# Moving the tiles of a tuned encoder layer to multiples of 512 bytes in SBUF

## The chip, the core and the metric

The kernel runs on one core of a Trainium2 chip. The metric is device time in microseconds, from the first to the last instruction of one execution with what lies around it; runs of one kernel are summed up by their median. SBUF is the on-chip memory: 128 partitions, each a strip of bytes. A tile lies at the same byte in every partition, and "place" below means that byte. TensorE (PE) multiplies matrices and loads the stationary operand of the next matmul (PEld) beside the running one; VectorE (DVE), ScalarE (ACT) and GpSimd (POOL) work on tiles; SyncE (SP) issues most DMAs.

## The reference

One encoder layer on 256 rows of width 2048, all in float32:

```
x <- LN1(alpha*x + 0.5*SwiGLU_1(x))      2048 -> 2 x 5632 -> 2048
x <- LN2(alpha*x + W_out [Hyena(x) ; DiffAttn(x)])
x <- LN3(alpha*x + 0.5*SwiGLU_2(x))
```

SwiGLU is `(silu(x Wg) * (x Wu)) Wd`. The mixer in the middle projects x by one matrix of 6144 columns: 3072 for Hyena (a short convolution, then two long convolutions whose filters come from a small sine network), 3072 for differential attention with 8 heads; both halves go through one output matrix. LN is a layer norm with gain and bias.

## The kernel before, in words

Every large product is made in float32r from operands that are split in two: a high part (a cast on ACT) and a low part (the rest, subtracted on DVE). Three products hi·hi, hi·lo and lo·hi stand for one float32 product.

All weights stream through SBUF in units of 512 KB, 128 x 1024 floats. `fetch` (L155) sends a unit into one of 4 buffers `raw`; `prepare` casts it into one of 4 buffers `whi` (names `hi...`, L171) and subtracts into one of 4 buffers `wlo` (names `lo...`, L172). The list `units` fixes their order, five units are fetched and two are prepared ahead of use. There are three kinds of stage:

- The gate stages (L368, L369) and the Hyena projection hold the activations `xx` (16 blocks of 2 x 256, high and low side by side) as the moving operand; a weight part is the stationary one. For each 128 columns of weights the high part meets all 512 columns of a block of `xx`, the low part the first 256.
- The down stages, the attention projection and the output projection (`mm3`, L90 to L92) hold a weight part as the moving operand, 512 columns, and `hh`/`hl` (or `xx`, `yhh`, `yah`) as the stationary one. In the last down stage four of the last eight units are prepared into `xx` itself, which is free by then, instead of `whi` and `wlo`.
- Beside these, generators that `tick` advances do the small work: the filter network (`filter_net`, L475 to L502) and the filters' spectra in the first FFN, the Hyena chains and the heads in the mixer. They take scratch tiles of 2 KB from a ring of eight, `t512`.

The order of instructions on each engine is the scheduler's: an instruction whose inputs are there early may be put far ahead of its place in the source. Tiles come from pools that lie one after the other in SBUF: `const`, `wp` (the units), `sm` (scratch), then the pools of a stage (`hh` and `hl`; `ssq`, `yah` and the rest of the mixer). A pool is filled in the order in which its tiles are first made, so every tile's size moves all that comes after it.

| tiles | place before | past a multiple of 512 | place now | past a multiple of 512 |
|---|---|---|---|---|
| `res` | 16512 | 128 | 18944 | 0 |
| `xx` | 32896 | 128 | 35328 | 0 |
| `ident`, `ones` | 65664, 66176 | 128 | 16896, 17408 | 0 |
| `pvt0`, `pvt1` | 66720, 67232 | 160 | 17920, 18432 | 0 |
| `raw` (4 of 4096) | from 67936 | 352 | from 68096 | 0 |
| `whi`, `wlo` (8 of 4096) | from 84320 | 352 | from 84480 | 0 |
| `t512` (8 of 2048) | from 117088 | 352 | from 117248 | 0 |
| `hf`, `sg` (4 of 1024) | from 133472 | 352 | from 134016 | 384 |
| `hh` | 139168 | 416 | 138752 | 0 |
| `hl` | 184224 | 416 | 183808 | 0 |
| mixer: `ssq`, `yah`, `yal`, `rope` | from 139168 | 416 | from 138752 | 0 |
| mixer: the rest (`qk`, `fw_hi`, `iv`, `yhh`, ...) | from 159712 | 480 | from 159232 | 0 |

Of the kernel before, what the change touches and what calls it, by code (L numbers as in the profile page):

```python
# [11 lines left out]
F32 = mybir.dt.float32  # L12
# [5 lines left out]
P = 128  # L18
# [9 lines left out]
EMB = 33  # L28
HID = 64
# [45 lines left out]
def kernel(ctx: ExitStack, tc: tile.TileContext, a: dict, out: bass.AP):  # L75
    nc = tc.nc

    const = ctx.enter_context(tc.tile_pool(name="const", bufs=1))
    wp = ctx.enter_context(tc.tile_pool(name="wp", bufs=4))
    sm = ctx.enter_context(tc.tile_pool(name="sm", bufs=2))  # L80
# [2 lines left out]

    def bank(name):
        return psp.tile([P, 512], F32, tag="ps", name=name)

    mm = nc.tensor.matmul

# [16 lines left out]
    def t512(name, shape=(2, CH)):  # L105
        return sm.tile([P, *shape], F32, tag="t512", name=name, bufs=T512)
# [105 lines left out]
            tick()  # L212


    res = const.tile([P, 2, D], F32, name="res")
    xx = const.tile([P, KD, 2, L], F32R, name="xx")
    xv = a["x"][0].rearrange("(p j) d -> p j d", j=2)
# [4 lines left out]
        if kp % 2 == 0:  # L222
            fetch(kp // 2 + 1)

    ident = const.tile([P, P], F32, name="ident")
    make_identity(nc, ident)
    ones = const.tile([P, P], F32, name="ones")
    nc.gpsimd.memset(ones, 1.0)
    mhalf = const.tile([P, 2], F32, name="mhalf")
    nc.gpsimd.memset(mhalf, -0.5)  # L230


    NCONV = 24
    NV = 4 * KD
    pvt = [const.tile([P, P], F32, name="pvt0"), const.tile([P, P], F32, name="pvt1")]

    def load_vectors():
        pv = [sm.tile([P, P], F32, tag="hf", name=f"pv{i}") for i in range(2)]
        for w in range(3):
            nc.gpsimd.dma_start(out=pv[0][w * NCONV:(w + 1) * NCONV, :], in_=a["hyena_conv_w"][0, w].rearrange("(t p) -> t p", p=P))  # L240
        nc.gpsimd.dma_start(out=pv[0][3 * NCONV:4 * NCONV, :], in_=a["hyena_conv_b"][0].rearrange("(t p) -> t p", p=P))
        r = 0
        for nme in ("ln1_g", "ln1_b", "ln2_g", "ln2_b"):
            nc.gpsimd.dma_start(out=pv[1][r:r + KD, :], in_=a[nme][0].rearrange("(t p) -> t p", p=P))
            r += KD
        nc.gpsimd.dma_start(out=pv[1][r:r + 8, :], in_=a["hyena_norm_g"][0].rearrange("(t p) -> t p", p=P))
        nc.gpsimd.dma_start(out=pv[1][r + 8:r + 9, :], in_=a["subln_g"])
        yield 4
        for i, n in ((0, 4 * NCONV), (1, NV + 9)):
            ps = bank(f"ps_pv{i}")  # L250
            nc.tensor.transpose(out=ps[:, :n], in_=pv[i][:n, :], identity=ident[:n, :n])
            nc.vector.tensor_copy(out=pvt[i][:, :n], in_=ps[:, :n])
# [11 lines left out]
    def xt_chunk(tag, c, g, b):  # L264
        for kp in (2 * c, 2 * c + 1):
            hs = xx[:, 2 * kp:2 * kp + 2, 0, :]
            ls = xx[:, 2 * kp:2 * kp + 2, 1, :]
            if g is None:
                i1 = nc.scalar.copy(out=hs, in_=xt0[kp])
                i2 = sub(nc.vector, ls, xt0[kp], hs)  # L270
                if c == 0:
                    hold["act"], hold["dve"] = i1, i2
                continue
            ps = bank(f"ps_xt{tag}_{kp}")
            for i in range(2):
                k = 2 * kp + i
                for j in range(2):
                    nc.tensor.transpose(out=ps[:, i * L + j * P:i * L + (j + 1) * P], in_=res[:, j, k * P:(k + 1) * P], identity=ident)  # L278
            t = t512(f"xt{tag}_{kp}")
            for i in range(2):  # L280
                k = 2 * kp + i
                i1 = nc.scalar.activation(out=t[:, i, :], in_=ps[:, i * L:(i + 1) * L], func=AF.Identity, bias=ln_col(b, k), scale=ln_col(g, k))  # L282
                if kp == 0:
                    nc.vector.tensor_copy(out=hs[:, i, :], in_=t[:, i, :])
                    i2 = sub(nc.vector, ls[:, i, :], t[:, i, :], hs[:, i, :])
            if kp > 0:
                nc.vector.tensor_copy(out=hs, in_=t)
                i2 = sub(nc.gpsimd if kp in (3, 5, 7) else nc.vector, ls, t, hs)
            if kp == 1:
                hold["act"], hold["dve"] = i1, i2  # L290

    def warm(n):

        ps = bank("ps_warm")
        for _ in range(n):
            mm(out=ps[:, :P], lhsT=ones, rhs=ones, start=True, stop=True)

    def scale_residual(tag, g, b):

        for c in range(4):  # L300
# [11 lines left out]
            for j in range(2):  # L312
# [2 lines left out]
                yield 1  # L315
                nc.vector.scalar_tensor_tensor(out=r, in0=bt, scalar=ALPHA, in1=r, op0=ALU.mult, op1=ALU.add)
                yield 1

    stats = const.tile([P, 2, 4, 6], F32, name="stats")

    def add_rows(ps, j, c, scale):
        cs = slice(c * 512, (c + 1) * 512)
# [150 lines left out]
    def filter_net():  # L473
        zt = t512("zt", (512,))[:EMB, :L]
        nc.sync.dma_start(out=zt, in_=a["c_zt"])  # L475
        w1 = sm.tile([EMB, HID], F32, name="w1", tag="w1", bufs=1)
        nc.sync.dma_start(out=w1, in_=a["filt_w1"][0])
        w2 = sm.tile([HID, HID], F32, name="w2", tag="w2", bufs=1)
        nc.sync.dma_start(out=w2, in_=a["filt_w2"][0])
        w3 = sm.tile([HID, 2, HID], F32, name="w3", tag="w3", bufs=1)  # L480
        fb = sm.tile([P, 4], F32, name="fb", tag="fb", bufs=1)
        for h in range(2):
            nc.sync.dma_start(out=w3[:, h, :], in_=a["filt_w3"][0])
            for i, nme in enumerate(("filt_b1", "filt_b2", "filt_b3", "filt_freq")):
                nc.gpsimd.dma_start(out=fb[h * HID:(h + 1) * HID, i:i + 1], in_=a[nme][0].rearrange("(h o) -> h o", o=1))
        yield 6

        def sine(o, ps, i, n, tag):
            ar = sm.tile([P, L], F32, tag="sg", name=f"ar{tag}")[:n]
            nc.vector.tensor_scalar(out=ar, in0=ps, scalar1=fb[:n, i:i + 1], scalar2=fb[:n, 3:4], op0=ALU.add, op1=ALU.mult)  # L490
            kn = sm.tile([P, L], F32, tag="hf", name=f"kn{tag}")[:n]
            nc.vector.tensor_scalar(out=kn, in0=ar, scalar1=1.0 / (2.0 * math.pi), scalar2=MAGIC, op0=ALU.mult, op1=ALU.add)
            nc.vector.tensor_scalar(out=kn, in0=kn, scalar1=-MAGIC, scalar2=None, op0=ALU.add)
            for c in (C1, C2, C3):
                nc.vector.scalar_tensor_tensor(out=ar, in0=kn, scalar=-c, in1=ar, op0=ALU.mult, op1=ALU.add)
            nc.vector.tensor_scalar(out=ar, in0=ar, scalar1=PI_LO, scalar2=-PI_LO, op0=ALU.min, op1=ALU.max)
            nc.scalar.activation(out=o, in_=ar, func=AF.Sin)

        h = zt
        for i, (w, n) in enumerate(((w1, HID), (w2, HID), (w3.rearrange("a b c -> a (b c)"), P))):  # L500
            ps = bank(f"ps_f{i}")
            mm(out=ps[:n, :L], lhsT=w, rhs=h, start=True, stop=True)  # L502
            h = t512(f"fh{i}", (512,))[:n, :L]
            yield 1
            sine(h, ps[:n, :L], i, n, f"f{i}")
            yield 3
        flt["h"] = h
# [97 lines left out]
    def rows_of_x():  # L605
# [4 lines left out]
        yield from scale_residual("0", None, None)  # L610

    ln = ffn("1", first0, filter_gen(), filter_net(), fill)
    xn1 = dr.tile([P, 2, D], F32, name="xn1")

# [13 lines left out]
    mixp = mix.enter_context(tc.tile_pool(name="mix", bufs=1, reuse_waits="tile"))  # L628
# [202 lines left out]
    yah = mixp.tile([P, 8, L], F32R, name="yah")  # L831
    yal = mixp.tile([P, 8, L], F32R, name="yal")
    rope = mixp.tile([P, 2, 2, 8, ROT], F32, name="rope")
    nlam = mixp.tile([P, 1], F32, name="nlam")
    g08 = mixp.tile([P, 1], F32, name="g08")

    def lambdas():
        nc.sync.dma_start(out=rope.rearrange("p a j g r -> p (a j g r)"), in_=a["c_rope"])
# [221 lines left out]
```

## Time and profile before

| | before |
|---|---|
| median of 3 runs | 1960.94 us (1959.08 to 1961.29) |
| the profiled execution | 1963.29 us, of it 1961.2 us span |
| granted TensorE clock, mean | 0.995 |
| PE busy | 1932.8 us, 99% of the span, 10260 matmuls |
| DVE, ACT, POOL busy | 62%, 47%, 16% |
| DMA moved | 376.43 MB, mean 192 GB/s |

A group's row of the profile reads: line, engine, operation, output<-inputs by the program's names, partitions x elements, count | busy us in all, mean ns of one | idle us just before and what ended it. Ends of matmuls are modelled, so their pace is better read from the starts in a timeline. In the table of waits a row says who waited for whom, us in all, how often, and the longest.

### The profile page before, as it was taken

What the parts mean: (1) busy time and instruction counts of PE and PEld (TensorE: products, weight loads), DVE (VectorE), ACT (ScalarE), POOL (GpSimd) and SP (SyncE); (2) the same over time, 40 slices, a digit from 0 to 9 for tenths busy, and PEclk for the clock granted to TensorE, in tenths of its full rate; (3) what the DMA queues carried; (4) which work ended last, traced back from release to release, by engine and by line L of the source; (5) the groups of instructions that cost most, each with busy time, mean ns of one, the idle gap of its engine ahead of it and who ended that gap; (6) DMA issues with size and microseconds to landing.
All of it is one profiled execution on the core that took longest, in us unless ns stands there. A gap on an engine that the chain in (4) does not pass through costs nothing. (4 is left out here: it accounts for less than half of the span.)

```text
span 1961.2 us, 27062 instructions
## 1 busy us (share of the span) xinstructions
PE 1932.8 (99%) x10260; PEld 1656.4 (84%) x10260; DVE 1215.4 (62%) x1538; ACT 926.1 (47%) x1334; POOL 305.3 (16%) x330
## 2 busy tenths in 40 slices
PE   9999999999999999999999999999999999999997
PEld 8888888888888887888887878888888888888885
DVE  5555556555566656899978666755555555544445
ACT  5554444544444435545555534545444544433332
POOL 4221111121100002012222011312111121100001
PEclk9999999999999999999999999999999999999999
DMA  8656656656666656655575444865656556555553
GB/s 288 204 187 192 190 189 198 192 185 193 203 208 214 204 191 207 220 181 153 172 226 161 158 154 157 274 191 187 192 191 193 187 189 194 187 189 187 189 186 115
DMA packets 294698, 376.43 MB, mean 192 GB/s; under 512 B 13263, under 2 KB 222312, under 8 KB 294568
## 3 DMA queue, kind: packets, MB, share of 16 engines
q1 hardware_dynamic: 289832, 361.90, 57.6%
q0 software_dynamic: 4736, 12.82, 2.2%
q8 instruction: 80, 1.31, 0.3%
q14 instruction: 50, 0.41, 0.1%
HBM read 366.27 MB, written 8.39 MB: 191 GB/s over the span
## 5 line engine op out<-in xcount | busy, mean ns | idle before, releaser
L368 PE MATMUL ps<-xx,hi1g 128*128 128x512 f32 x1408 | 490.2, 391 | 1.5 <-ACT hi1g L171 1.5
L368 PE MATMUL ps<-xx,hi2g 128*128 128x512 f32 x1408 | 488.6, 390 | 1.1 <-DVE xx L95 1.1
L369 PE MATMUL ps<-xx,lo1g 128*128 128x256 f32 x1408 | 397.4, 283 | 0.1
L369 PE MATMUL ps<-xx,lo2g 128*128 128x256 f32 x1408 | 397.0, 282 | 0.0
L172 DVE TENSOR_TENSOR lo2g<-raw2g,hi2g 128x1024 fp32r<-128x1024 f32 x176 | 234.8, 1335 | 179.6 <-ACT hi2g L171 179.6
L172 DVE TENSOR_TENSOR lo1g<-raw1g,hi1g 128x1024 fp32r<-128x1024 f32 (+1 forms) x178 | 232.5, 1308 | 177.6 <-ACT hi1g L171 177.6
L368 PEld LDWEIGHTS ps<-xx,hi1g 128*128 128x128 f32 x1408 | 264.8, 188 | 58.2 <-ACT hi1g L171 1.7
L368 PEld LDWEIGHTS ps<-xx,hi2g 128*128 128x128 f32 x1408 | 264.3, 188 | 56.4 <-ACT xt L282 1.3
L171 ACT CAST hi2g<-raw2g 128x1024 fp32r<-128x1024 f32 x176 | 185.0, 1052 | 187.3 <-PE ps L368 174.9
L171 ACT CAST hi1g<-raw1g 128x1024 fp32r<-128x1024 f32 (+1 forms) x178 | 185.2, 1042 | 179.7 <-PE ps L368 170.7
L369 PEld LDWEIGHTS ps<-xx,lo1g 128*128 128x128 f32 x1408 | 266.7, 190 | 0.7 <-DVE lo1g L172 0.5
L369 PEld LDWEIGHTS ps<-xx,lo2g 128*128 128x128 f32 x1408 | 266.1, 189 | 0.1
L404 POOL TENSOR_TENSOR hf<-hf,sg 128x256 f32<-128x256 f32 x88 | 64.7, 755 | 741.8 <-DVE hf L373 741.7
L172 DVE TENSOR_TENSOR lo2d<-raw2d,hi2d 128x1024 fp32r<-128x1024 f32 x84 | 103.6, 1233 | 118.7 <-ACT hi2d L171 118.7
L171 ACT CAST hi1d<-raw1d 128x1024 fp32r<-128x1024 f32 x88 | 92.4, 1050 | 132.0 <-PE pd L92 119.7
L171 ACT CAST hi2d<-raw2d 128x1024 fp32r<-128x1024 f32 x84 | 88.4, 1052 | 138.7 <-PE pd L92 131.0
L172 DVE TENSOR_TENSOR lo1d<-raw1d,hi1d 128x1024 fp32r<-128x1024 f32 x88 | 107.2, 1221 | 72.7 <-ACT hi1d L171 72.7
L90 PE MATMUL pd<-hi1d,hh 128*128 128x512 f32 x352 | 139.3, 396 | 0.0
L368 PE MATMUL ph<-xx,hihy 128*128 128x512 f32 x384 | 137.0, 397 | 2.2 <-DVE xx L95 1.1
L92 PE MATMUL pd<-hi1d,hl 128*128 128x512 f32 x352 | 139.1, 395 | 0.0
L91 PE MATMUL pd<-lo1d,hh 128*128 128x512 f32 x352 | 139.1, 395 | 0.0
L90 PE MATMUL pd<-hi2d,hh 128*128 128x512 f32 x336 | 132.9, 395 | 0.0
(380 smaller groups left out, 3078.8 us busy)
## 6 DMA issues: line engine op xcount, KB each, us to landing
raw1d<-in_ffn_w_down_dram SPq DMA_DIRECT2D x88, 512.0 KB, 4.3
raw2g<-in_ffn_w_gate_dram SPq DMA_DIRECT2D x88, 512.0 KB, 3.5
raw2g<-in_ffn_w_up_dram SPq DMA_DIRECT2D x88, 512.0 KB, 3.5
raw2d<-in_ffn_w_down_dram SPq DMA_DIRECT2D x88, 512.0 KB, 4.2
raw1g<-in_ffn_w_gate_dram SPq DMA_DIRECT2D x87, 512.0 KB, 3.5
raw1g<-in_ffn_w_up_dram SPq DMA_DIRECT2D x87, 512.0 KB, 3.9
rawhy<-in_w_in_dram SPq DMA_DIRECT2D x48, 512.0 KB, 4.5
rawat<-in_w_in_dram SPq DMA_DIRECT2D x48, 512.0 KB, 4.2
```

The lines of the kernel that those rows point to most:

```text
L90: mm(out=o, lhsT=lh, rhs=rh, start=start, stop=False)
L91: mm(out=o, lhsT=lh, rhs=rl, start=False, stop=False)
L92: mm(out=o, lhsT=ll, rhs=rh, start=False, stop=stop)
L171: i1 = nc.scalar.copy(out=hi[:, s_], in_=raw[:, s_])
L172: i2 = nc.vector.tensor_tensor(out=lo[:, s_], in0=raw[:, s_], in1=hi[:, s_].bitcast(F32), op=ALU.subtract)
L368: mm(out=ps[t], lhsT=h[:, k, ts_], rhs=xx[:, kk].rearrange("p a l -> p (a l)"), start=kk == 0, stop=False)
L369: mm(out=ps[t][:, :L], lhsT=lo[:, k, ts_], rhs=xx[:, kk, 0, :], start=False, stop=kk == KD - 1)
L404: nc.gpsimd.tensor_tensor(out=hf, in0=hf, in1=sg, op=ALU.mult)
```

## The change

No arithmetic is changed. The constants that are small (`mhalf`, `stats`) and those of 512 bytes (`ident`, `ones`, the two `pvt`) are made first, with a spacer behind the small ones; the spacers `space` are tiles that nothing reads or writes. `sm` gets a spacer of 384 bytes, which makes its length such that the next pool begins on a multiple of 512. Three tiles of the filter network (`w1`, `w2`, `w3`, 256, 256 and 512 bytes) become pieces of one scratch tile `fw` of the ring `t512`. `nlam` and `g08`, 4 bytes each, go from the mixer's pool to `sm`.

```diff
+    def line(pool, n):
+
+        pool.tile([P, n // 4], F32, name="space", tag="space", bufs=1)
...
+    mhalf = const.tile([P, 2], F32, name="mhalf")
+    stats = const.tile([P, 2, 4, 6], F32, name="stats")
+    line(const, 384 - 32 - 192)
+    ident = const.tile([P, P], F32, name="ident")
+    ones = const.tile([P, P], F32, name="ones")
+    pvt = [const.tile([P, P], F32, name="pvt0"), const.tile([P, P], F32, name="pvt1")]
...
     res = const.tile([P, 2, D], F32, name="res")
     xx = const.tile([P, KD, 2, L], F32R, name="xx")
...
-    ident = const.tile([P, P], F32, name="ident")
+    line(sm, 384)
     make_identity(nc, ident)
-    ones = const.tile([P, P], F32, name="ones")
     nc.gpsimd.memset(ones, 1.0)
-    mhalf = const.tile([P, 2], F32, name="mhalf")
     nc.gpsimd.memset(mhalf, -0.5)
...
-    pvt = [const.tile([P, P], F32, name="pvt0"), const.tile([P, P], F32, name="pvt1")]
...
-    stats = const.tile([P, 2, 4, 6], F32, name="stats")
...
-        w1 = sm.tile([EMB, HID], F32, name="w1", tag="w1", bufs=1)
+        ws = t512("fw", (512,))
+        w1, w2 = ws[:EMB, :HID], ws[:HID, HID:2 * HID]
+        w3 = ws[:HID, 2 * HID:4 * HID].rearrange("p (a b) -> p a b", a=2)
         nc.sync.dma_start(out=w1, in_=a["filt_w1"][0])
-        w2 = sm.tile([HID, HID], F32, name="w2", tag="w2", bufs=1)
         nc.sync.dma_start(out=w2, in_=a["filt_w2"][0])
-        w3 = sm.tile([HID, 2, HID], F32, name="w3", tag="w3", bufs=1)
...
-    nlam = mixp.tile([P, 1], F32, name="nlam")
-    g08 = mixp.tile([P, 1], F32, name="g08")
+    nlam = sm.tile([P, 1], F32, name="nlam", tag="nlam", bufs=1)
+    g08 = sm.tile([P, 1], F32, name="g08", tag="g08", bufs=1)
```

On four engines the order of instructions stays as it was. On DVE one instruction moves: the product that makes `g08` (printed as `g`) from a column of `pvt`. Before, its tile shared bytes with the first FFN's `hh`, and it stood at the end of that FFN, between the sum of the last rows and their statistics:

```order
L323 SCALAR_TENSOR_TENSOR res<-pd_3_1_6239,res 128x512 [waits PE_49]
L851 TENSOR_SCALAR g_8514<-pvt_107 128x1 [waits Pool_49]
L324 BN_STATS stats<-res 128x6 [waits DVE_49]
L328 BN_AGGR mv_6678<-stats 128x2 [waits DVE_49]
L330 TENSOR_SCALAR rs_6680<-mv_6678 128x1 [waits DVE_49]
```

Now it stands near the start of the program, right behind the copy that fills `pvt`, in front of the low part of a unit:

```order
L261 COPY pvt_74<-ps_pv_404 128x96 [waits PE_49]
L261 COPY pvt_75<-ps_pv_407 128x73 [waits PE_49]
L858 TENSOR_SCALAR g_8514<-pvt_75 128x1 [waits DVE_49]
L176 TENSOR_TENSOR lo1g_2_0_429<-raw1g_2_0_330,hi1g_2_0_428 128x1024 [waits DMAHW6_49,Activation_49]
L380 TENSOR_TENSOR hf_0_366<-ps_0_1_0_136,hf_0_366 128x256 [waits DMASW2_49,DMASW1_49,DMASW3_49,DMASW0_49,Activation_49]
```

The rows at the end of the first FFN are otherwise as before.

## The prediction, made before the changed kernel was run

> **What bounds the kernel now.** I read the page's busy table and its groups first, then the table by stage, then the waits of PE, and last single stretches of the timeline. The profiled execution took 1963.29 us, 2.35 us over the median of the runs (1960.94); its span is 1961.2 us, and 2.1 us lie around it.
>
> ```profile
> PE 1932.8 (99%) x10260; PEld 1656.4 (84%) x10260; DVE 1215.4 (62%) x1538; ACT 926.1 (47%) x1334; POOL 305.3 (16%) x330
> ```
>
> The table by stage (us, then busy us of each engine with its count, granted clock, DMA share, GB/s) has PE without a gap in both FFNs:
>
> ```profile
> 0.00:60.00 60.00, 57.31 (x313) 50.73 (x314) 36.23 (x41) 34.22 (x49) 31.62 (x42) 0.97 0.87 278
> 60.00:630.00 570.00, 570.00 (x3141) 495.79 (x3140) 330.23 (x368) 272.06 (x390) 84.41 (x94) 1.00 0.61 195
> 630.00:760.00 130.00, 130.00 (x577) 105.61 (x576) 72.35 (x77) 52.34 (x55) 3.20 (x7) 1.00 0.61 197
> 760.00:960.00 200.00, 192.53 (x1126) 169.65 (x1125) 180.90 (x335) 109.54 (x176) 39.36 (x34) 0.98 0.59 187
> 960.00:1210.00 250.00, 245.97 (x1217) 201.27 (x1216) 181.38 (x306) 119.37 (x210) 41.20 (x41) 1.00 0.54 173
> 1210.00:1870.00 660.00, 660.00 (x3567) 571.68 (x3566) 365.73 (x365) 311.85 (x431) 97.19 (x107) 1.00 0.61 195
> 1870.00:1961.00 91.00, 76.95 (x330) 61.63 (x328) 48.57 (x51) 26.77 (x26) 8.28 (x6) 0.95 0.44 148
> ```
>
> So PE is idle for 28 us: 2.7 at the head, 11.5 in the mixer (7.5 + 4.0), 14 at the end. The rest, 1933 us, is the pace of the matmuls, and only that pace is large enough to be measured in this kernel: 0.2% of the time, which I take as the least that can be told from no change, is 3.9 us, or 0.38 ns on each of 10260 matmuls. The question is whether a place in SBUF changes that pace.
>
> **The change, part by part: the matmuls.** The kernel before already has operands at four different places: 128 bytes past a multiple of 512 (`xx`), 352 (the units), 416 (`hh`, `hl`) and 480 (most of the mixer). If place mattered, like operations should differ between them. The groups, kept apart by shape:
>
> ```profile
> L91 PE MATMUL pd<-lo2d,hh 128*128 128x512 f32 x336 | 132.9, 395 | 0.0
> L91 PE MATMUL pd<-xx,hh 128*128 128x512 f32 x16 | 6.3, 395 | 0.0
> L90 PEld LDWEIGHTS pd<-hi2d,hh 128*128 128x128 f32 x336 | 63.2, 188 | 15.3
> L90 PEld LDWEIGHTS pa0k<-hiat,xx 128*128 128x128 f32 x32 | 6.0, 188 | 1.4
> L91 PEld LDWEIGHTS pwo<-lowo,yhh 128*128 128x128 f32 x64 | 12.1, 189 | 2.6
> L368 PEld LDWEIGHTS ps<-xx,hi2g 128*128 128x128 f32 x1408 | 264.3, 188 | 56.4 <-ACT xt L282 1.3
> ```
>
> A stationary operand loads in 188 or 189 ns from 416, 128, 480 and 352 alike. For the moving operand the ends are modelled, so I take the starts. In the last down stage 24 matmuls read a unit that was prepared into `xx` (128), the next 24 one from the ordinary buffers (352), and then 24 from `xx` again:
>
> ```profile
> 1924.41 0.40 PE L90 MATMUL pd<-xx,hh 128*128 128x512 f32 x1
> 1930.00 0.40 PE L90 MATMUL pd<-hi2d,hh 128*128 128x512 f32 x1
> 1935.60 0.40 PE L90 MATMUL pd<-xx,hh 128*128 128x512 f32 x1
> 1941.20 0.39 PE L90 MATMUL pd<-hi2d,hh 128*128 128x512 f32 x1
> ```
>
> 5.59, 5.60 and 5.60 us for 24 each: 0.233 us for one, and a difference of at most 0.01 us in 24, 0.4 ns each. 128 is a multiple of 64 and 352 is not, so any rule with pieces of up to 32 bytes, or of 64, is seen to cost nothing. What no row shows is a start on a whole 512 (or 256): all four places cross one more such border than an aligned operand does. The cost of that crossing has to be bounded. From above in time: nothing lost. From below: at most what separates the slower matmuls from the faster ones, which I price as a rival. The nearest rows are the three stretches just shown, so I take 0, with 0.4 ns each way as the plain uncertainty: 3072 matmuls of 512 columns in the down, attention and output products (2112, 576 and 384 by the loops) by 0.4 ns are 1.2 us, and over all 10260 it would be 4.1 us.
>
> [...]
>
> **DVE, ACT and POOL.** Their operations move with their operands:
>
> ```profile
> L172 DVE TENSOR_TENSOR lo1d<-raw1d,hi1d 128x1024 fp32r<-128x1024 f32 x88 | 107.2, 1221 | 72.7 <-ACT hi1d L171 72.7
> L172 DVE TENSOR_TENSOR xx<-raw2d,xx 128x1024 fp32r<-128x1024 f32 x4 | 4.9, 1221 | 1.7 <-ACT xx L171 1.6
> L171 ACT CAST hi2d<-raw2d 128x1024 fp32r<-128x1024 f32 x84 | 88.4, 1052 | 138.7 <-PE pd L92 131.0 <-DMA raw2d<-in_ffn_w_down_dram 4.3 <-PE ps L368 3.5
> L171 ACT CAST xx<-raw2d 128x1024 fp32r<-128x1024 f32 x4 | 4.2, 1052 | 2.2 <-DMA raw2d<-in_ffn_w_down_dram 2.2
> ```
>
> Writing to 352 or to 128 takes the same 1221 and 1052 ns. Even a change here would lie beside PE: DVE idles for 42 to 45 of every 100 us in the FFNs, and ACT waits mostly for PE to free the weight buffers. In the mixer, where DVE is busy for 181 of 200 us, a change of 1% in its operations would move the 7.5 idle us of PE by up to 1.8 us; I take 0.
>
> **The transfers.** Rows of 1 to 2 KB now land at whole multiples of 512. If they came faster, it would show where PE waits for a unit or its input. These are the waits of PE, whole:
>
> ```profile
> PE py L90 <- ACT rha L98: 1.9, 1, 1.9
> PE pw L923 <- DVE e L919: 1.6, 1, 1.6
> PE py L91 <- DVE rla L95: 1.5, 1, 1.5
> PE ps L368 <- ACT hi1g L171: 1.5, 1, 1.5
> ...
> PE ph L369 <- DVE lohy L172: 0.5, 1, 0.5
> ```
>
> Only the 1.5 us at the head has a transfer behind it (the first unit). A tenth off the 3.5 us (its row is below) in which a gate unit lands is 0.35 us, so the gain is 0 to 0.4 us; I take 0.1. With the cover gone it would be one landing per unit, but the covers are five units of lead.
>
> ```profile
> raw2g<-in_ffn_w_gate_dram SPq DMA_DIRECT2D x88, 512.0 KB, 3.5
> ```
>
> **The moved instruction.** `g08` leaves the end of the first FFN, where PE goes idle for the statistics:
>
> ```profile
> 760.65 0.69 DVE L323 SCALAR_TENSOR_TENSOR res<-pd,res 128x512 f32<-128x512 f32 x1 [0.49 <-PE pd L92]
> 761.38 0.69 DVE L324 BATCH_NORM_STATS2 stats<-res 128x6 f32<-128x512 f32 x1
> 763.45 0.69 DVE L323 SCALAR_TENSOR_TENSOR res<-pd,res 128x512 f32<-128x512 f32 x1 [0.89 <-PE pd L92]
> 764.05 0.14 DVE L851 TENSOR_SCALAR g<-pvt 128x1 f32<-128x1 f32 x1
> 764.17 0.69 DVE L324 BATCH_NORM_STATS2 stats<-res 128x6 f32<-128x512 f32 x1
> ```
>
> From the sum to the statistics it is 0.73 us for the other half of the rows, without `g08`, and 0.72 with it: it sat in the wait of the statistics for the sum, so its removal gives 0, at most 0.14. Where it goes now, DVE has 0.18 us of waiting for ACT, and what is queued behind it is the low part of a unit that PE uses two units later:
>
> ```profile
> 35.71 0.39 DVE L252 COPY pvt<-ps_pv 128x96 f32<-128x96 f32 x2
> 36.28 1.23 DVE L172 TENSOR_TENSOR lo1g<-raw1g,hi1g 128x1024 fp32r<-128x1024 f32 x1 [0.18 <-ACT hi1g L171]
> ```
>
> Cost there: 0 to 0.14 us on DVE, 0 on PE.
>
> **The filter's weights in the ring.** `fw` is one more tile in a ring of eight, so the scratch tiles of the filters' side work change places and a few of their waits. It is side work of the first FFN, whose stages have PE busy in 570 of 570 and 130 of 130 us. I take 0, with 0.5 us each way for its three small matmuls, which stand in PE's own row. The spacers cost nothing: no instruction touches them.
>
> **The sum**: matmuls 0 (up to 1.2 us each way, 4.1 at the very most), transfers −0.1 (−0.4 to 0), side work 0 (0.5 each way), the mixer 0 (1.8 each way), `g08` 0 (−0.14 to 0). From 1963.29 the profiled execution would go to 1963.2, and the median from 1960.9 to 1960.8; no change beyond what can be told. The runs before span 2.2 us by themselves.
>
> **The rivals.** A, faster: crossings cost something and go. Starts give a price. Gate pairs (512 and 256 columns), and matmuls of 256 columns alone:
>
> ```profile
> 299.87 0.39 PE L368 MATMUL ps<-xx,hi1g 128*128 128x512 f32 x1
> 301.95 0.39 PE L368 MATMUL ps<-xx,hi1g 128*128 128x512 f32 x1
> 763.24 0.28 PE L90 MATMUL prk<-xx 128*128 128x256 f32 x1
> 765.40 0.28 PE L90 MATMUL pik<-xx 128*128 128x256 f32 x1
> ```
>
> Six pairs in 2.08 us are 0.347 each; 18 matmuls of 256 columns in 2.16 are 0.120 each; so 512 columns take 0.227 in a gate, where the moving tile lies at 128, and 0.233 in a down stage, where it lies at 352. If that 6 ns were the place, 3072 by 6 ns, 18 us, would go: 1942. Against it stand the 24 with a moving operand at 128 that run at 0.233 too. For it: nothing but that 512 itself is untried. Chance 0.09, somewhat smaller gains included. [...]
>
> B, slower: operands that began at different places within 512 bytes now begin at the same one, and the load of the stationary operand meets the reading of the moving one in the same part of the memory. The place is the gate stage (`xx` at 128 against units at 352 before, both at 0 now). The price is the slower pace that the kernel knows, 0.233 for 0.227: 3200 pairs of the gates and of Hyena's projection (2816 and 384) by 6 ns, 19 us, 1980; it decides from 1.2 ns a pair. Against it: `prk<-xx` above has both operands in `xx`, at equal places already, and its 256 columns take 0.120 us, only 3 ns over half of the 0.233 that 512 take with operands at 416 and 352. Chance 0.07.
>
> C, the transfers or the mixer's chains change by more than I give them: 1 to 3 us either way, 1958 to 1964, still no change. Chance 0.10.
>
> D, the places do not become what the change says: `hf` and `sg` in fact stay 384 past a multiple of 512. They only feed DVE, ACT and POOL, so the time is the same; it is part of the forecast.
>
> **How the numbers follow.** Forecast 0.69 (with D), C 0.10, A 0.09, B 0.07, and 0.05 for effects of unknown sign. Same: the forecast and nearly all of C, 0.77; faster: A and half of the unknown, 0.13; slower 0.10. The likeliest case alone lies in 1958 to 1964. The range is 1954 to 1966: it takes in C and the smaller effects on either side, and leaves out A and B at full size, under 2 in 10.
>
> **What would show it.** Right: the groups L368 to L369 and L90 to L92 at 390, 283 and 395 ns as before, starts 0.347 and 0.233 apart, LDWEIGHTS at 188, PE busy near 1933. A shows as a down pace below 0.233, B as a gate pair above 0.347. Transfers show in the median landing of `raw2g` against 3.5 us, with PE's waits unchanged. I am wrong if the pace of the matmuls moves by more than 0.4 ns each.

## The result, and the profile after

The changed kernel takes 1947.22 us (median of 4 runs, 1945.09 to 1950.04) where the kernel before took 1961.12 beside it (4 runs, 1959.08 to 1962.32): a ratio of 0.9931, with an interval of 0.9914 to 0.9948. It is faster by 13.9 us, where no change was forecast, and lies outside the range of 1954 to 1966. The profiled execution, from which all that follows is read, took 1945.09 us against 1963.29: 18.2 us less, with a span of 1943.3 us against 1961.2 and the same mean clock of 0.996 and 0.995.

The busy table and two rows of the table by stage, same windows and columns as before:

```profile
PE 1914.9 (99%) x10260; PEld 1644.5 (85%) x10260; DVE 1215.8 (63%) x1538; ACT 927.2 (48%) x1334; POOL 305.3 (16%) x330
```

```profile
60.00:630.00 570.00, 570.00 (x3153) 495.91 (x3152) 331.34 (x369) 273.66 (x391) 85.07 (x95) 1.00 0.62 197
630.00:760.00 130.00, 130.00 (x604) 108.79 (x602) 75.53 (x87) 51.58 (x54) 3.88 (x7) 1.00 0.61 198
```

PE's busy time fell by 17.9 us, which is what the span lost; that of the loads (PEld) fell by 11.9 us, and those of DVE, ACT and POOL are those of before. PE is still without a gap in 570 of 570 and 130 of 130 us, at a clock of 1.00, but 604 matmuls instead of 577 fall into the window of the first down stage (in its last 3 us the next stage has begun). So no wait went away; the matmuls themselves go faster, and not in all stages: 200 us of the second FFN's gates hold 1156 before (first row) and 1156 now (second row).

```profile
1400.00:1600.00 200.00, 200.00 (x1156) 177.31 (x1155) 109.99 (x109) 97.29 (x144) 34.33 (x36) 1.00 0.60 190
```

```profile
1400.00:1600.00 200.00, 200.00 (x1156) 174.85 (x1155) 110.03 (x109) 97.49 (x145) 34.39 (x36) 1.00 0.60 190
```

In the groups (mean ns of one behind the comma) the down products changed from 395 to 390 ns, and the gates' two forms moved against each other (390 and 282 before, 394 and 277 now in the second FFN):

```profile
L375 PE MATMUL ps<-xx,hi2g 128*128 128x512 f32 x1408 | 488.6, 394 | 1.1 <-DVE xx L99 1.1
L376 PE MATMUL ps<-xx,lo2g 128*128 128x256 f32 x1408 | 390.0, 277 | 0.0
...
L95 PE MATMUL pd<-lo1d,hh 128*128 128x512 f32 x352 | 137.2, 390 | 0.0
...
L176 DVE TENSOR_TENSOR lo1d<-raw1d,hi1d 128x1024 fp32r<-128x1024 f32 x88 | 107.2, 1222 | 66.0 <-ACT hi1d L175 66.0
...
L175 ACT CAST hi2d<-raw2d 128x1024 fp32r<-128x1024 f32 x84 | 88.6, 1055 | 130.6 <-PE pd L96 124.0 <-PE ps L375 3.4 <-DMA raw2d<-in_ffn_w_down_dram 3.2
...
L95 PEld LDWEIGHTS pd<-lo1d,hh 128*128 128x128 f32 x352 | 66.1, 188 | 13.3
```

Casts, subtractions and loads of stationary operands take what they took (1052, 1221 and 188 ns before). The starts give the pace. In the last down stage, two rows of the timeline that lie 21 matmuls apart:

```profile
1907.16 0.39 PE L94 MATMUL pd<-xx,hh 128*128 128x512 f32 x1
...
1911.92 0.39 PE L94 MATMUL pd<-xx,hh 128*128 128x512 f32 x1
```

4.76 us for 21 are 0.2267 each, where 24 took 5.60, 0.233 each. The same done for all matmuls, by summing the intervals from each start to the next (in the means, intervals over 260 ns, and pairs over 400, are left out, since they hold a wait; the sums hold them):

| product | matmuls | ns of one, before | now | sum, us |
|---|---|---|---|---|
| down (`pd`), 512 columns | 2111 | 233.2 | 226.9 | −13.5 |
| attention (`pa`), 512 | 576 | 233.0 | 228.4 | −2.5 |
| output (`pwo`), 512 | 384 | 232.8 | 228.2 | −1.7 |
| gates (`ps`), pairs of 512 and 256 | 2816 pairs | 346.7 | 346.8 | +0.2 |
| Hyena's projection (`ph`), same pairs | 384 pairs | 346.9 | 352.4 | +0.1 |
| the rest | | | | −0.5 |

That is −17.9 us from PE's first start to its last. The gain sits in the 3072 matmuls whose stationary operand is an activation and whose moving one is a weight: 17.7 us together, 5.8 ns each. The gates kept their sum but with another split, 231 and 116 ns for 228 and 119. In Hyena's projection the pace became slower, and shorter waits made that good.

The remaining rows that the prediction named: the landing of a gate unit, the wait of the first gate, and `g08` (printed as `g`) at its new place on DVE.

```profile
raw2g<-in_ffn_w_gate_dram SPq DMA_DIRECT2D x88, 512.0 KB, 3.4
```

```profile
PE ps L375 <- ACT hi1g L175: 2.6, 1, 2.6
```

```profile
36.08 0.39 DVE L261 COPY pvt<-ps_pv 128x96 f32<-128x96 f32 x2
36.51 0.15 DVE L858 TENSOR_SCALAR g<-pvt 128x1 f32<-128x1 f32 x1
36.59 1.23 DVE L176 TENSOR_TENSOR lo1g<-raw1g,hi1g 128x1024 fp32r<-128x1024 f32 x1
```

None of them holds anything of the gain: 3.4 for 3.5 us, 1.1 us more at the head, and 0.15 us on DVE with PE busy.

### The profile page after: what moved, and what is told of

It is laid out like the page before. It is cut to its first block, busy times and chain, and to the rows that moved or that the text cites. A ratio compares the mean times of both kernels' runs of the same rounds, so it can differ in the third digit from the quotient of the medians.

```text
span 1943.3 us, 27060 instructions
## 1 busy us (share of the span) xinstructions
PE 1914.9 (99%) x10260; PEld 1644.5 (85%) x10260; DVE 1215.8 (63%) x1538; ACT 927.2 (48%) x1334; POOL 305.3 (16%) x330
## 5 line engine op out<-in xcount | busy, mean ns | idle before, releaser
L376 PE MATMUL ps<-xx,lo2g 128*128 128x256 f32 x1408 | 390.0, 277 | 0.0
L176 DVE TENSOR_TENSOR lo2g<-raw2g,hi2g 128x1024 fp32r<-128x1024 f32 x176 | 235.4, 1339 | 179.0 <-ACT hi2g L175 179.0
L176 DVE TENSOR_TENSOR lo1g<-raw1g,hi1g 128x1024 fp32r<-128x1024 f32 (+1 forms) x178 | 232.8, 1309 | 177.6 <-ACT hi1g L175 177.2
```

Source lines behind the costliest of these rows:

```text
L176: i2 = nc.vector.tensor_tensor(out=lo[:, s_], in0=raw[:, s_], in1=hi[:, s_].bitcast(F32), op=ALU.subtract)
L376: mm(out=ps[t][:, :L], lhsT=lo[:, k, ts_], rhs=xx[:, kk, 0, :], start=False, stop=kk == KD - 1)
```

## The experiments

The first theory after the result was that the *distance* between a matmul's two operands sets its pace (place of the stationary one minus place of the moving one), and that equal places are fast. Its rival is the prediction's own A: each operand is read faster when it begins on a multiple of 512. Places are given below as bytes past a multiple of 512, in the order `xx` / units / `hh` with the mixer's tiles. Before they were 128 / 352 / 416 and 480, after the change 0 / 0 / 0.

### Everything at 352

The small tiles of `const` get a spacer more, so that all large tiles lie at 352 / 352 / 352: off the multiples of 512, but at equal places.

```diff
+    line(const, 352, "space1")
     res = const.tile([P, 2, D], F32, name="res")
```

> All large tiles 352 bytes past a multiple of 512: no operand begins on a multiple of 512 (or 64), but all begin at the same one. Theory S (each operand must itself begin on a whole multiple): the down, attention and output matmuls go back to 0.233 us from start to start, and the time to about 1961. Theory D (only the distance between the two operands of a matmul counts): 0.227 us and about 1947, as with all at 0.

Measured: 1945.68 us (2 runs), before 1962.19 (21 runs), ratio 0.9917, 0.9889 to 0.9946. The window of 640 to 740 us lies in the first down stage; before, after, and this kernel:

```profile
640.00:740.00 100.00, 100.00 (x444) 81.24 (x443) 56.44 (x62) 41.61 (x45) 2.11 (x4) 1.00 0.60 195
```

```profile
640.00:740.00 100.00, 100.00 (x456) 83.33 (x455) 58.08 (x63) 42.52 (x45) 2.11 (x4) 1.00 0.61 199
```

```profile
640.00:740.00 100.00, 100.00 (x455) 83.31 (x454) 57.98 (x62) 42.18 (x46) 2.11 (x4) 1.00 0.65 200
```

455 matmuls in 100 us as with the change, where before had 444; the starts give 226.9 ns in the down stages. The whole gain is there without one large tile on a multiple of 512, so the alignment is not what does it.

### Only `hh` and the mixer moved away

```diff
-    line(sm, 384)
+    line(sm, 288)
```

This gives 0 / 0 / 416.

> xx and the units at multiples of 512, the stage pools (hh, hl, the mixer's tiles) 416 past one. S with the stationary operand at fault, or D: down matmuls 0.233 (2112 of them, so 13 us back, about 1960), attention matmuls (xx against units) 0.227. S with the moving operand at fault: 0.227 everywhere, about 1947.

Measured: 1964.88 us (8 runs, 1959.53 to 1967.87), ratio 1.0013, 1.0000 to 1.0026. The same window, and the group of one attention product, which reads `xx` and units alone:

```profile
640.00:740.00 100.00, 100.00 (x444) 81.14 (x443) 56.90 (x61) 41.78 (x45) 2.10 (x4) 1.00 0.63 195
```

```profile
L96 PE MATMUL pa0k<-loat,xx 128*128 128x512 f32 x32 | 12.4, 389 | 0.0
```

The down stage is back at 444 (233.3 ns), with the moving operand still on a multiple of 512. The attention products, whose operands both stayed at 0, kept the fast 389 ns.

### Only the units moved away

```diff
     xx = const.tile([P, KD, 2, L], F32R, name="xx")
+    line(const, 352, "space2")
...
-    line(sm, 384)
+    line(sm, 32)
```

This gives 0 / 352 / 0, and all the small edits (`fw`, `g08`, `nlam`, the order of the constants) stay in.

> xx and the stage pools at multiples of 512, the units (moving in the down, attention and output products, stationary in the gates) 352 past one. S with the moving operand at fault, or D: down, attention and output matmuls 0.233, about 1961. S with the stationary operand at fault: those 0.227, and only the gate pairs (0.347) could grow; about 1947.

Measured: 1961.33 us (8 runs), ratio 0.9995, 0.9984 to 1.0007.

```profile
640.00:740.00 100.00, 100.00 (x444) 81.16 (x443) 56.62 (x62) 41.85 (x45) 2.10 (x4) 1.00 0.64 194
```

Nothing is left of the gain: the down and the attention products are at 233.2 and 233.3 ns. So the small edits are together worth nothing that can be measured, and `hh` on a multiple of 512 by itself is worth nothing either.

### Only `xx` moved away

`res` and `xx` are made first, so that `xx` lies at 128 as before and the units and `hh` at 0.

```diff
+    res = const.tile([P, 2, D], F32, name="res")
+    xx = const.tile([P, KD, 2, L], F32R, name="xx")
     mhalf = const.tile([P, 2], F32, name="mhalf")
...
-    res = const.tile([P, 2, D], F32, name="res")
-    xx = const.tile([P, KD, 2, L], F32R, name="xx")
```

> res and xx 128 past a multiple of 512 as in the kernel before, units and stage pools at multiples. Down matmuls 0.227 by every theory. S with the stationary operand, or D: attention matmuls (stationary xx) 0.233, 3.7 us back, about 1951. S with the moving operand: attention 0.227, but the 48 last matmuls that move xx 0.233. In the gates 0.347 a pair by all.

Measured: 1959.53 us (8 runs), ratio 0.9984, 0.9973 to 0.9996: nearly the whole gain is gone, although the down stages kept it. The window of the down stage, and one in the gates of the second FFN:

```profile
640.00:740.00 100.00, 100.00 (x457) 83.38 (x456) 59.48 (x66) 42.36 (x46) 2.61 (x5) 1.00 0.66 200
...
1400.00:1600.00 200.00, 200.00 (x1141) 175.49 (x1140) 108.48 (x108) 96.43 (x144) 34.37 (x36) 1.00 0.62 187
```

The changed kernel had 1156 matmuls in the same window of the gates (above). 1141 for 1156 are 351.1 ns a pair, 4.3 more than with the change; over 2816 pairs that is 12 us. This was missed: the gates had been expected to go at 0.347 us whatever the distance, and the kernel at about 1951. Their pace too differs with the distance, but by another table, since they had been as fast at 224 (before, 346.7) as at 0 (346.8).

### PE alone, by distance

To get that table, a kernel that leaves out the whole layer: `x` is copied to the output, and PE multiplies pieces of it, 192 matmuls in a row for each distance `d`, with a new stationary operand for every matmul and no other engine at work.

```python
for i in range(n):
    s = deltas[i % len(deltas)] // 4 + 128 * (i % 6)
    c = cols[i % len(cols)]
    m = shift // 4 + 512 * (i % 4)
    mm(out=ps[:, :c], lhsT=st[:, s:s + 128], rhs=mv[:, m:m + c], start=i == 0, stop=i == n - 1)
```

> No layer is computed: after x is loaded and copied into two float32r tiles, PE runs groups of 192 matmuls back to back with nothing beside it, one group per distance (bytes, stationary less moving operand), names q (512 columns), g (512 and 256 in turn), h (256); the output is x. Theory D (distance alone, within PE's own two reading streams): q000 and q512 at 0.227 us from start to start, every distance that occurs in the runs so far (64, 128, 160, 288, 384, 416) near 0.233; both64 and both352 (both operands shifted alike) 0.227; moved64 0.233; g064 or g384 over 0.347 a pair. If instead other engines or DMA writes had to meet PE's reading, all groups run at 0.227. Open: whether 256, 32, 16 and 4 bytes count as a distance.

Groups of 512 columns; the number in the name is the distance, and the busy time by 192 is the pace to within 1 ns (it holds the tail of the last matmul). `both352` has both operands at 352, `moved64` the moving one at 64 and the stationary one at 0:

```profile
L101 PE MATMUL q000w<-mv,st 128*128 128x512 f32 x192 | 43.7, 389 | 0.0
...
L101 PE MATMUL q004w<-mv,st 128*128 128x512 f32 x192 | 44.8, 394 | 0.0
...
L101 PE MATMUL q064w<-mv,st 128*128 128x512 f32 x192 | 45.0, 396 | 0.0
...
L101 PE MATMUL q192w<-mv,st 128*128 128x512 f32 x192 | 44.1, 391 | 0.0
...
L101 PE MATMUL q256w<-mv,st 128*128 128x512 f32 x192 | 43.7, 389 | 0.0
...
L101 PE MATMUL both352w<-mv,st 128*128 128x512 f32 x192 | 43.7, 389 | 0.0
...
L101 PE MATMUL moved64w<-mv,st 128*128 128x512 f32 x192 | 44.1, 391 | 0.0
```

Mean intervals from start to start, ns:

| distance | 0, 256, 512 | 4 | 16, 32, 64 | 96, 352 | 128, 160 | 192, 448 | 224, 288 to 320, 384 to 416, 480 |
|---|---|---|---|---|---|---|---|
| 512 columns | 226.66 | 232.38 | 233.33 to 233.35 | 234.24 | 233.35 | 228.94 | 233.31 to 233.36 |

| distance | 0 | 32, 64 | 352 | 128, 384 | 192 | 224, 480 | 256 | 448 |
|---|---|---|---|---|---|---|---|---|
| pair of 512 and 256 columns | 353.2 | 353.3, 353.2 | 346.7 | 351.0, 351.2 | 353.4 | 346.8 | 353.2 | 348.9 |

256 columns alone take 120.0 at 0 and 256, and 117.8 at 64. Three things follow. The loss needs nothing but PE and its two operands, since nothing else ran. For 512 columns it is all or nothing in most cases: 6.7 ns at most distances, 5.7 already at 4 bytes, and none at multiples of 256; at 352 for both operands it is again none (226.8). And `moved64`, at a distance of −64, for which 0.233 us had been expected, goes at 228.95, where distance 192 has 228.94; and 0, 256 and 512, 96 and 352, 128 and 384, 192 and 448 each share one pace to within 0.05 ns. So in these rows of 512 columns the distance modulo 256 tells the pace, with its sign. (For the pairs, 192 and 448 are equal modulo 256 and still differ, 353.4 and 348.9; a later run shows two rhythms of pairs at 0 and at 256, and none was made of pairs at 192.)

With this table the places of before can be read: the down products lay at a distance of 64 (416 − 352), those of the units in `xx` at 288, the attention at −224, the output products at 64 and 128. At all of these PE alone takes 233.3 or 233.4 ns. The gates lay at 224 (352 − 128), the fast one for pairs.

### A distance of 256

This kernel has 352 / 96 / 352: distances of 256 everywhere, and no equal places.

```diff
-    line(const, 384 - 32 - 192)
...
+    line(const, 256, "space2")
...
-    line(sm, 384)
+    line(sm, 128)
```

> xx and the stage pools at equal places (352 past a multiple of 512), the units 256 bytes away from both. D with a period of 512: down, attention and output matmuls 0.233, about 1960. D with a period of 256: 0.227 and about 1947. The 48 last matmuls that move xx (distance 0) 0.227 by both.

Measured: 1948.35 us (4 runs, 1944.17 to 1952.94), before 1962.41 (5 runs), ratio 0.9922, 0.9897 to 0.9946. The down products go at 226.9 ns and the attention at 228.4, as with the change: 256 is as good as 0. The gates show something else, in an early and a late window; then the early one of the changed kernel:

```profile
100.00:280.00 180.00, 180.00 (x1021) 156.02 (x1020) 96.46 (x96) 85.74 (x126) 30.55 (x32) 1.00 0.61 186
...
1400.00:1600.00 200.00, 200.00 (x1156) 174.90 (x1155) 110.00 (x109) 97.43 (x144) 34.44 (x36) 1.00 0.61 190
```

```profile
100.00:280.00 180.00, 180.00 (x1040) 158.73 (x1039) 99.50 (x98) 88.84 (x133) 33.07 (x35) 1.00 0.61 190
```

1021 matmuls for 1040 early, 353.3 ns a pair, and then 1156 in the late window as the changed kernel has, 346.7. The same operands at the same distance have two rhythms. The gates took 4.8 us more here than in the changed kernel, of the 7.8 us that the two spans differ by.

### One of three stationary operands displaced

The change as it is, with `hl` 64 bytes further. In each three matmuls of the down stages two read `hh` and one reads `hl`.

```diff
             hh = fp.tile([P, KF, L], F32R, name=f"hh{tag}")
+            fp.tile([P, 16], F32, name="space")
             hl = fp.tile([P, KF, L], F32R, name=f"hl{tag}")
```

> As the changed kernel, but hl begins 64 bytes past a multiple of 512 (hh at 0), in both FFNs: in a down stage one of three matmuls (the third, hl) has its stationary operand at distance 64. If a matmul is slowed by its own operand's distance, the third of each three takes 0.233 from its start to the next, the others 0.227. If it is slowed by the load that runs beside it (the next stationary operand), it is the second of each three. Either way a third of the 13.6 us of the down stages is lost: about 1951.

Measured: 1960.75 us in one run, span 1959.0. Two rows of the timeline, five threes apart, and the first matmul of each three and the displaced one as groups:

```profile
1880.11 0.39 PE L94 MATMUL pd<-hi2d,hh 128*128 128x512 f32 x1
...
1883.57 0.39 PE L94 MATMUL pd<-hi2d,hh 128*128 128x512 f32 x1
```

```profile
L96 PE MATMUL pd<-hi1d,hl 128*128 128x512 f32 x352 | 139.7, 397 | 0.0
...
L94 PE MATMUL pd<-hi1d,hh 128*128 128x512 f32 x352 | 137.2, 390 | 0.0
```

3.46 us by 5 are 0.692 a three (693.4 ns over all of them), 12.7 more than the 680.6 of the change, out of the 19.1 between it and before. A third of the loss had been expected, 1951 us, in the interval of one matmul; two thirds came back, from one operand of three, and all three intervals grew: to 235.4 for the displaced matmul, 229.3 for the one before it and 228.6 for the one behind it. The down stages cost 9.0 us more than with the change. The early gates went at the slow rhythm besides, 6.1 us more; that part has nothing to do with `hl`, which is not read there, so only the 9.0 us belong to the displaced operand.

### Gates at 224 and the down stages at 0

The places that the table gives as good for both: 128 / 352 / 352. The attention is then at 32, a slow distance.

```diff
+    res = const.tile([P, 2, D], F32, name="res")
+    xx = const.tile([P, KD, 2, L], F32R, name="xx")
     mhalf = const.tile([P, 2], F32, name="mhalf")
     stats = const.tile([P, 2, 4, 6], F32, name="stats")
-    line(const, 384 - 32 - 192)
...
-    res = const.tile([P, 2, D], F32, name="res")
-    xx = const.tile([P, KD, 2, L], F32R, name="xx")
```

> Places chosen by distance alone: xx 128 past a multiple of 512, units and stage pools 352, so that the gates and the Hyena projection keep 224 and the down and output products get 0 (attention 32). By the table of distances: gate and Hyena pairs 0.347 without the slower stretches of the changed kernel, down and output 0.227, attention 0.233. Against the kernel before 2112 and 384 matmuls at 6.7 ns less, 16.7 us: about 1945; against the changed kernel 3 us lost in the attention, up to 2.5 won in the Hyena projection, more where its gates run in the slow rhythm.

Measured: 1948.23 us (4 runs, 1946.03 to 1948.97), before 1962.02 (6 runs), ratio 0.9933, 0.9915 to 0.9951. A window in Hyena's projection before, after, and here:

```profile
800.00:850.00 50.00, 50.00 (x308) 45.01 (x309) 45.51 (x86) 28.50 (x46) 2.99 (x2) 1.00 0.64 203
```

```profile
800.00:850.00 50.00, 50.00 (x306) 44.31 (x305) 44.95 (x82) 27.24 (x44) 7.83 (x6) 1.00 0.59 189
```

```profile
800.00:850.00 50.00, 50.00 (x310) 45.08 (x309) 44.99 (x82) 27.77 (x44) 7.78 (x6) 1.00 0.60 189
```

The pairs go at 346.7 to 347.0 ns from end to end, in the gates and in Hyena's projection, and the down products at 227.1. The attention pays 2.7 us for it, at 233.2 ns:

```profile
L95 PE MATMUL pa0k<-loat,xx 128*128 128x512 f32 x32 | 12.7, 395 | 0.0
```

### The changed kernel again, beside it

The kernel of the change itself, unaltered, in the same series as the one above.

> The changed kernel itself once more beside the other, same chip and rounds. About 1947 with a wider spread, if its gates at distance 0 fall into one of two rhythms (0.347 or 0.353 a pair) from execution to execution.

Measured: 1944.79 us (4 runs, 1942.87 to 1945.30), ratio 0.9912, 0.9897 to 0.9928. So the kernel above, 3.4 us slower, is no improvement on it, where about 1945 had been expected of it; against the kernels before, both gain 14 to 17 us. In the run profiled here, the gates kept the fast rhythm, but for a stretch from 307 to 318 us (353.3 ns a pair), and Hyena's projection went at 351.9. Over the whole projection that costs 0.2 us against the kernel above and not the 1.9 of the paces, since the waits were shorter. The wider spread that had been thought possible did not come: the four runs cover 2.4 us.

### The two rhythms, PE alone

Again without the layer and with `x` as output. Six stretches of 64 pairs each at one distance, with 1 to 5 small matmuls between one stretch and the next, to see whether a disturbance changes the rhythm.

```python
for r in range(6):
    for i in range(64):
        s, m = d // 4 + 128 * (i % 6), 512 * (i % 4)
        mm(out=ps, lhsT=st[:, s:s + 128], rhs=mv[:, m:m + 512], ...)
        mm(out=ps[:, :256], lhsT=st[:, s + 128:s + 256], rhs=mv[:, m:m + 256], ...)
    for _ in range(r + 1):
        mm(out=pk[:, :128], lhsT=st[:, :128], rhs=mv[:, :128], start=True, stop=True)
```

> No layer is computed: PE alone, groups as in the run of distances; output is x. k groups: 6 times 64 gate pairs at one distance, with 1 to 5 short matmuls between the stretches. If distance 0 (and 256) has two rhythms, some stretches run at 0.347 a pair and some at 0.353, while 224 and 96 always run at 0.347. p groups: high and low stationary part at two distances (p000x224: 512 columns at 0, 256 at 224). one064: each sixth matmul at 64, the others at 0: about 0.2278 on the mean if the loss of 6.7 ns belongs to single matmuls; the interval that grows tells whether it is the matmul's own operand or the load beside it. t groups: 384 columns.

Starts 18 pairs apart at distance 0, in the first stretch and in the fourth:

```profile
24.36 0.39 PE L110 MATMUL k000w<-mv,st 128*128 128x512 f32 x1
...
30.72 0.40 PE L110 MATMUL k000w<-mv,st 128*128 128x512 f32 x1
...
94.59 0.39 PE L110 MATMUL k000w<-mv,st 128*128 128x512 f32 x1
...
100.83 0.39 PE L110 MATMUL k000w<-mv,st 128*128 128x512 f32 x1
```

6.36 by 18 are 0.3533, 6.24 by 18 are 0.3467. By stretch, at the end of each: 353.6, 353.5, 353.5, 346.6, 353.6, 346.7 at distance 0; 346.6, 353.0, 346.6, 353.0, 346.6, 346.6 at 256; and 346.6 or 346.7 in all six at 224 and at 96. So the stretches at 0 and 256 ended at one of two rhythms, 346.6 or 353.0 to 353.6, and those at 224 and 96 all at the fast one. That fits the early gates of the kernel with distances of 256 and the Hyena pairs of the changed kernel. It also fits where the rhythm changes in the layer: in the six profiled kernels whose gates lie at a distance of 0 or 256, the first FFN's pairs from 20 us on are either at 346.7 or at 353.3 ns, and pass from one to the other only where a few other matmuls stand among them (in the changed kernel the transposes that fill `pvt` near 35 us, and the filter network's near 293, 305 and 317 us); the 744 pairs between the first two of these places keep their rhythm.

In the same run one operand of six was displaced in rows of 512-column matmuls, by 64, 32 and 128 bytes:

```profile
L101 PE MATMUL one064w<-mv,st 128*128 128x512 f32 x192 | 44.3, 392 | 0.0
L101 PE MATMUL one032w<-mv,st 128*128 128x512 f32 x192 | 44.3, 392 | 0.0
L101 PE MATMUL one128w<-mv,st 128*128 128x512 f32 x192 | 44.1, 391 | 0.0
```

With 128 bytes its own interval was 234.3 ns, that of the matmul just before it 232.3, and the other four 226.7: 13 ns for one displaced operand. With 64 bytes its own was 235.9, and the three behind it took 228.2, 232.8 and 231.1; with 32 bytes the one before it took 235.0, its own 229.0, and the two behind it 232.0 and 231.0. That is 20 ns for one displaced operand in both, a mean of 230.05 and 229.97 over the row, where about 227.8 had been expected at 64. In the run by distance, with every second operand at 64, the mean was 230.03, some 7 ns for each displaced one. So the cost is not that of a fixed number of intervals: at 64 bytes it is 20 ns for one in six, 13 for one in three (the kernel with `hl` moved) and 7 for one in two.

Some rows of pairs had their high part at one distance and their low part at another. High at 224 and low at 0 took 344.5 ns a pair, 2.2 less than the best row with one distance for both; high at 0 and low at 224 took 353.3. These are single rows of 96 pairs, and no run has them in the layer. Rows of 384 columns took 173.4 and 173.3 ns at 8 and 64, 176.0 at 128 and 176.7 at 224: a third shape, and again another table.

### The runs together

Distances modulo 256, and the paces measured in the layer beside those of PE alone:

| places `xx` / units / `hh` | gates: distance, ns a pair | down: distance, ns | attention: distance, ns |
|---|---|---|---|
| before, 128 / 352 / 416 | 224, 346.7 | 64, 233.2 | 32, 233.0 |
| change, 0 / 0 / 0 | 0, 346.8 | 0, 226.9 | 0, 228.4 |
| 352 / 352 / 352 | 0, 346.9 | 0, 226.9 | 0, 228.4 |
| 0 / 0 / 416 | 0, 346.9 | 160, 233.3 | 0, 228.8 |
| 0 / 352 / 0 | 96, 346.7 | 160, 233.2 | 160, 233.3 |
| 128 / 0 / 0 | 128, 351.1 | 0, 227.0 | 128, 232.4 |
| 352 / 96 / 352 | 0, 353.3 then 346.7 | 0, 226.9 | 0, 228.4 |
| 128 / 352 / 352 | 224, 346.7 | 0, 227.1 | 32, 233.2 |
| PE alone | 0: 353.6 or 346.6; 96, 224: 346.6; 128: 351.0 | 0: 226.7; 64, 160: 233.4 | 0: 226.7; 32, 128, 160: 233.3 to 233.4 |

Every row of the layer is that of PE alone at its distances, to within 1 ns or, for the attention, some 2 (its 228 holds the starts of its units, some of them 235 ns).

## Why the prediction was wrong, point by point

- **The step that failed is the first term of the sum: "matmuls 0 (up to 1.2 us each way, 4.1 at the very most)".** It measured −17.7 us on the 3072 matmuls that the term counted. It rested on "If place mattered, like operations should differ between them." The three stretches of 24 were such a pair, but what differed between them was the place of the moving operand; their distances were 32 and 64 modulo 256, and PE alone takes 233.34 and 233.35 ns at these. Both sides of the comparison were slow. The rule drawn from it, that a place costs nothing, was a statement on distances that had not been in the sample: among the products of 512 columns with a weight moving, none lay at a multiple of 256 before. The prediction saw that a start on a whole 512 was in no row, and took it as a crossing of a border by one operand; a relation between the two operands it priced for the gate pairs alone, as rival B.
- **The 188 ns of the loads was no test.** LDWEIGHTS takes 188 ns in the down groups after the change as before, and in the runs of PE alone a median of 188 at distance 64 as at 0. The loss shows in the intervals between the starts of matmuls, 233.2 ns for 226.9 in the down stages.
- **Rival A had the size and not the mechanism.** 6 ns on 3072, 18 us, 1942: measured were 5.8 ns, 17.7 us and 1944.79 to 1947.22. But the starts on multiples of 512 are not what gained: with everything at 352 the gain is whole, and where only the stationary or only the moving operand of the down products lies on a multiple of 512 nothing of it remains in them. The reason held against it ("24 with a moving operand at 128 that run at 0.233 too") counted against the crossing and was silent on the distance. The price itself came from taking 0.120 out of a gate pair's 0.347; that gave 0.227, the true fast pace, by luck: PE alone at the gates' distance of 224 takes 233.3 for 512 columns by themselves, and the pairs have their own table.
- **Rival B was right that operands at equal places touch the pairs, and wrong in size.** Hyena's pairs went from 346.9 to 352.4 ns, 2 us which shorter waits gave back; the gates held 346.8 in the run profiled. It is a second rhythm, 353.5 ns in the run of PE alone where other stretches at the same distance had 346.6, and not 6 ns on every pair. The evidence against it (`prk`, 256 columns at 120 ns in equal places) was a shape which shows little: 120.0 at 0 and 117.8 at 64. A lasting loss in the gates came at a distance of 128 (12 us), which the change did not take.
- **DVE, ACT, transfers, `g08`, the filter's ring, the spacers: nothing that can be measured, as forecast.** Their rows are those of before, but for 1.1 us more of waiting at the head, and the kernel with the units alone moved away, which has all the small edits, takes 0.9995 of the time before.
- **The table by stage was read rightly**: PE without a gap, 1933 us of pace, and the pace the only thing large enough. The sign that would show the error, a move of the pace by more than 0.4 ns, was the right one too. What was too narrow was the range: the only bound on an untried place was taken from places like the one left.

What stays open: why the distance sets the pace; the runs show that it does and not by what. With 128 bytes the interval of the displaced matmul grows (234.3 ns) and that of the one before it (232.3), beside which its operand is loaded (in the changed kernel's down stage the load of the matmul that starts at 700.22 us runs from 700.00 to 700.19, beside the one that starts at 700.00); with 64 and 32 bytes intervals behind it grow too (228.2 to 232.8), and the runs do not say why. The scatter of runs at distance 0 (four runs with distances of 256 spread over 8.8 us, eight of 0 / 0 / 416 over 8.3, where the 21 of before cover 5.8) would follow from the two rhythms of the gates, which two profiles show, of the kernel with distances of 256 and of the one with `hl` displaced; the profiled run of 0 / 0 / 416, 1960.28 us with its gates at 346.9, lies near the lower end of its eight, and the longer ones have no profile, so that is argued; and the four runs of the changed kernel in its second series, which cover 2.4 us, show that a distance of 0 need not scatter. Attention at 0 with gates at 224 would need the attention's units 32 bytes away from the other units, and it was not tried.

## What to carry to other kernels

Where PE has no gaps, take the interval from start to start by product and compare it with the fastest that the same shape reaches anywhere; here 233.3 ns for a shape that took 226.7 elsewhere, both at a granted clock of 1.00, had a cause, and the distance between the two operands modulo 256 bytes is one to check, before any multiple of a large number. By PE alone, products of 512 columns with a new stationary operand each were fastest at 0 and 256 (226.7 ns), and alternating pairs of 512 and 256 had the fast rhythm in every stretch at 96 and 224 (346.6 or 346.7) but not at 0 and 256, so that with one distance for all units no place of `xx` that was run is sure to serve both. And a comparison that shows "no effect" bounds only what it varied: ask of each pair of rows which relation between the operands, not only which address, stayed the same.

## What the runs showed of the hardware that was not expected

- With PE alone, the pace of float32r matmuls of 512 columns with a new stationary operand each went with the distance of their operands modulo 256 bytes: 226.66 ns at 0, 233.3 to 234.2 at nearly all others that were run, 228.94 at 192, and 232.38 at only 4 bytes. The sign counted: 64 took 233.3 ns, −64 took 228.95, as 192 did.
- One displaced operand in six cost more than its own interval: 13 ns with 128 bytes (234.3 and 232.3 for 226.7), 20 with 64 or 32. In the layer one in three at 64 brought back two thirds of the loss, 693.4 ns where 680.6 and 699.7 are the ends.
- The same instructions on the same operands had two rhythms at distances 0 and 256, 346.6 and 353.0 to 353.6 ns a pair with PE alone; in the first FFN of the six profiled kernels at these distances they passed from one to the other (346.7 and 353.3) only where a few other matmuls stood among the pairs. At 96 and 224 all six stretches had the fast one.
